# Neighbourhood attention on one Trainium2 core: a head's bias joins its mask by an accumulating transfer instead of an addition on GpSimd

## The chip, the core and the metric

The kernel runs on one core of one Trainium2 chip. The metric is the device time of one execution in microseconds (us); less is better. The core has TensorE (PE in the profile; PEld is its weight load), VectorE (DVE), ScalarE (ACT), GpSimd (POOL) and SyncE (SP). SP, ACT and POOL can issue transfers (DMAs), which 16 DMA engines carry out.

## What is computed

One pre-norm encoder block in float32 on 512 tokens of width 2048: a combined input projection, two attention mixers side by side (eight heads of latent attention, MLA, and eight heads of neighbourhood attention on an 8 by 64 grid), an output projection, a squared-ReLU MLP of width 8192 and a last norm. The change is in the neighbourhood attention, whose reference is, cut to what matters:

```
def na_mixer(q, k, v, rpb):
    ...
    dr = rs + jnp.arange(kr) - r + (NA_ROWS_MAX - 1)
    bias = rpb[:, dr[:, None, None], dc[None, :, :]]
    ...
    s = jnp.einsum('bchd,bicjhd->bhcij', qr, kw, ...) * scale
    s = (s + bias[None]).reshape(B, H, W, kr * kc)
    p = jax.nn.softmax(s, axis=-1)...
    return jnp.einsum('bhcij,bicjhd->bchd', p, vw)
```

A query sees 16 columns of all 8 grid rows, with a learned bias for each relative position and head.

## The kernel before, in words

The tokens are laid out column by column, so that a block of 128 queries covers 16 grid columns and needs at most 256 keys. The window is a mask of zeros and -1e30 with three variants (left edge, middle, right edge): a constant array `mask` of 128 x 3 x 256 numbers. The bias of a head is one 128 x 256 array; all eight lie in a DRAM tensor `b_d`, which 8 + 16 transfers on POOL's queue put together from the weights at the start (lines 277 and 279).

For each head `na_load` (from line 440) fetches the head's q, k and v blocks, its bias into `bt` (line 451) and the mask into `bm` (line 453), all from SP's queue, and GpSimd then adds the bias to each of the three mask variants, in place in `bm` (line 454). `bt` and `bm` have one buffer each. `na_steps` then works on four query blocks. Step `s1`: the score matmul (line 470), then VectorE scales the scores and adds `bm` (line 472), takes the row maximum (475), ScalarE exponentiates (476), VectorE takes the reciprocal and normalises (477, 478). Step `s2` transposes the probabilities on TensorE (483) and ScalarE copies them out (485). Step `s3` multiplies them with v (492); after the fourth block `finish_head` scales the head's output, and GpSimd adds its squares to a running sum (509).

The order is made by hand and then by the framework. By hand: the heads' steps are tasks, and `hook()` runs those that are due after each product of a Strassen-like projection (`strassen_t`, lines 305 to 307, seven products for each of twelve weight blocks, 24 matmuls of 256 columns each). A head's load is due three hooks ahead of its first `s1`, its blocks follow every second hook, and `s2` comes two or three hooks after `s1`. So the attention runs in the gaps of the projection, from about 107 to 404 us; the last two heads lie beside the MLA set-up (lines 549 to 594: transposes of the latents, rope, and the projections `mq`, `mk`, `mvp` of lines 102 to 104). Then, when the kernel is built, the framework fixes one order for each engine and each queue: it takes what it estimates to be ready first, earlier statements before later ones, and puts in the waits. Each engine works through its own list in order, so one that waits holds up all that stands behind it.

Helpers have one line for all callers: `split` writes each float32 operand as a high and a low part (ACT line 92, DVE line 93), `TT` is a VectorE operation on two tensors (line 204), and `raw_unit` is a weight load (line 77).

Of the kernel before, what the change touches and what calls it, by code (L numbers as in the profile page):

```python
# [10 lines left out]
F32 = mybir.dt.float32  # L11
F32R = mybir.dt.float32r
AF = mybir.ActivationFunctionType
ALU = mybir.AluOpType
# [3 lines left out]
P = 128  # L18
# [18 lines left out]
def block_kernel(ctx, tc, x, xT, w_c, w_ckv, w_qkv, w_uqn, w_uqr, w_ukv, rpb, gcols, w_out, w_ff1, w_ff2, g_fin,  # L37
                 cs, mask, out):
    nc = tc.nc
# [4 lines left out]
    def open_pool(name, bufs=1, **kw):  # L44
        e = ExitStack()
        p = e.enter_context(tc.tile_pool(name=name, bufs=bufs, **kw))
        stacks[name] = e
        return p
# [166 lines left out]
    for k in range(KH):  # L215
        xt = load_xT(k) if k else xt0
        for j in range(2):
            sc = nc.vector.scalar_tensor_tensor(out=xt[:, 2 * j:2 * j + 2], in0=xt[:, 2 * j:2 * j + 2],
                                                scalar=gc[:, G_IN + k + KH * j:G_IN + k + KH * j + 1],
                                                in1=rB3 if k else rt_.rearrange("p (b n) -> p b n", b=2), op0=ALU.mult, op1=ALU.mult)  # L220
# [50 lines left out]
    b_d = tc.dram_tile([P, H, 256], F32, name="b_d")  # L271
# [6 lines left out]
    for ql in range(16):  # L278
        nc.gpsimd.dma_start(out=b_d[ql * 8:(ql + 1) * 8],
                            in_=g_d[:, :, 15 - ql:47 - ql, :].rearrange("q h c r -> q h (c r)"))  # L280
# [148 lines left out]
    na = open_pool("na", side="left")  # L429
# [10 lines left out]
    def na_load(h):  # L440
        p, h2 = h // 2, h % 2
        if p == 3:
            qT, kT = (last[w][:, h2 * S:(h2 + 1) * S] for w in range(2))
        else:
            qT, kT = (na.tile([P, S], F32, name=f"n{t}{h}", tag=f"n{t}", bufs=1) for t in "qk")
            nc.sync.dma_start(out=qT, in_=q_d[p][:, h2 * S:(h2 + 1) * S])
            nc.sync.dma_start(out=kT, in_=k_d[p][:, h2 * S:(h2 + 1) * S])
        vn = na.tile([P, NM, P], F32, name=f"nvn{h}", tag="nv", bufs=2)
        nc.sync.dma_start(out=vn, in_=v_d[p].rearrange("p (m d) -> p m d", m=NM)[:, :, h2 * P:(h2 + 1) * P])
        bt = na.tile([P, 256], F32, name=f"bt{h}", tag="bt", bufs=1)  # L450
        nc.sync.dma_start(out=bt, in_=b_d[:, h, :])
        bm = na.tile([P, 3, 256], F32, name=f"bm{h}", tag="bm", bufs=1)
        nc.sync.dma_start(out=bm, in_=mask)
        nc.gpsimd.tensor_tensor(out=bm, in0=bm, in1=bt.unsqueeze(1).broadcast_to([P, 3, 256]), op=ALU.add)
        return h, qT, kT, vn, bm

    def na_steps(h, t0, gap):
        d = {}

        def start():  # L460
            d["in"] = na_load(h)
# [723 lines left out]
```

## Time and profile before

| what | us |
|---|---|
| median of 3 runs | 1959.23 (1957.66 to 1959.66) |
| the profiled execution | 1961.26 |
| its span, first to last instruction | 1959.50 |
| what lies around the span | 1.76 |
| TensorE busy | 1941.2 (99%) |
| VectorE busy | 1567.3 (80%) |
| ScalarE busy | 1004.3 (51%) |
| GpSimd busy | 63.2 (3%) |
| DMA queue of SP, share of 16 engines | 41.4% |

The profile records one execution. Busy shares are means over the whole span; waits and the timeline tell what a stretch is limited by. In the timeline a row has the start, the duration, the engine, the line, the operation, and output <- inputs; the bracket at its end is the idle time of the engine ahead of it and what ended that. Matmuls overlap, so their durations are longer than their spacing.

### The profile page before, as it was taken

What the parts mean: (1) busy time and instruction counts of PE and PEld (TensorE: products, weight loads), DVE (VectorE), ACT (ScalarE), POOL (GpSimd) and SP (SyncE); (2) the same over time, 40 slices, a digit from 0 to 9 for tenths busy, and PEclk for the clock granted to TensorE, in tenths of its full rate; (3) what the DMA queues carried; (4) which work ended last, traced back from release to release, by engine and by line L of the source; (5) the groups of instructions that cost most, each with busy time, mean ns of one, the idle gap of its engine ahead of it and who ended that gap; (6) DMA issues with size and microseconds to landing.
All of it is one profiled execution on the core that took longest, in us unless ns stands there. A gap on an engine that the chain in (4) does not pass through costs nothing.

```text
span 1959.5 us, 31084 instructions
## 1 busy us (share of the span) xinstructions
PE 1941.2 (99%) x12510; PEld 1765.3 (90%) x12510; DVE 1567.3 (80%) x1894; ACT 1004.3 (51%) x1436; POOL 63.2 (3%) x69
## 2 busy tenths in 40 slices
PE   9999999999999999999999999999999999999998
PEld 8999999888887899999999999998888888888886
DVE  8677777787535687787878787875899999999996
ACT  5654555575314555555555555555454454454443
POOL 2100010100000000000000000000000000000000
PEclk9999999999999999999999999999999999999999
DMA  8354554431334344545454545357355345444433
GB/s 285 131 195 142 174 165 149 138 113 49 101 120 164 127 151 140 173 145 179 142 182 140 183 135 189 130 168 251 129 189 174 132 161 165 168 161 132 159 134 135
DMA packets 121936, 303.75 MB, mean 155 GB/s; under 512 B 10816, under 2 KB 49728, under 8 KB 121536
## 3 DMA queue, kind: packets, MB, share of 16 engines
q1 hardware_dynamic: 98416, 271.09, 41.4%
q10 hardware_dynamic: 22608, 29.52, 4.2%
q8 instruction: 98, 1.61, 0.3%
q0 software_dynamic: 768, 1.15, 0.2%
q14 instruction: 46, 0.38, 0.1%
HBM read 250.60 MB, written 52.26 MB: 155 GB/s over the span
## 4 chain that ended last, share of the span: by engine, by line
PE 94%; DVE 2%; ACT 1%; DMA 1%; issue 1%; POOL 0%; POOLq 0%; DVEq 0%; ACTq 0%; SPq 0%
PE px L307 8%; PE px L306 8%; PE px L305 8%; PE sx L1000 5%; PE sx L1002 5%; PE sx L1001 5%; PE pz L307 4%; PE pz L306 4%; PE pz L305 4%; PE wo L104 3%; PE wo L102 3%; PE wo L103 3%; PE sz L1000 3%; PE sz L1002 3%; PE sz L1001 3%; PE py L307 2%
## 5 line engine op out<-in xcount | busy, mean ns | idle before, releaser
L92 ACT CAST op_a<-sb 128x1024 fp32r<-128x1024 f32 x58 | 61.1, 1053 | 61.7 <-PE sx L1002 23.8
L93 DVE TENSOR_TENSOR op_a<-sb,op_a 128x1024 fp32r<-128x1024 f32 x58 | 70.3, 1217 | 6.6 <-ACT op_a L92 6.6
L204 DVE TENSOR_TENSOR SF<-SF,sx 128x1024 f32<-128x1024 f32 x56 | 67.9, 1212 | 0.6 <-PE sx L1002 0.6
L204 DVE TENSOR_TENSOR sb<-sb,sb 128x1024 f32<-128x1024 f32 x56 | 67.1, 1218 | 0.5
L92 ACT CAST s_0hi<-sb 128x1024 fp32r<-128x1024 f32 x28 | 29.5, 1055 | 42.6 <-PE sx L1002 16.8
L127 POOL TENSOR_TENSOR stat<-stat,nhalf 128x1 f32<-128x1 f32 (+1 forms) x6 | 7.3, 1217 | 1355.7 <-DVE stat L126 1355.7
L92 ACT CAST a_0hi<-sb 128x1024 fp32r<-128x1024 f32 x27 | 28.5, 1055 | 35.1 <-PE sz L1002 16.6
L886 ACT ACTIVATE v<-v 128x512 f32<-128x512 f32 x64 | 40.4, 631 | 3.1 <-DVE v L204 2.2
L887 ACT ACTIVATE v<-v 128x512 f32<-128x512 f32 x64 | 40.6, 634 | 1.9
L92 ACT CAST a_1hi<-sb 128x1024 fp32r<-128x1024 f32 x27 | 28.4, 1051 | 23.3 <-PE sz L1002 10.0
L93 DVE TENSOR_TENSOR a_0lo<-sb,a_0hi 128x1024 fp32r<-128x1024 f32 x27 | 32.9, 1219 | 8.8 <-ACT a_0hi L92 8.8
L92 ACT CAST s_1hi<-sb 128x1024 fp32r<-128x1024 f32 x28 | 29.4, 1050 | 17.0 <-PE sx L1002 16.7
L204 DVE TENSOR_TENSOR b<-b,b 128x1024 f32<-128x1024 f32 x31 | 37.6, 1214 | 0.0
L93 DVE TENSOR_TENSOR s_0lo<-sb,s_0hi 128x1024 fp32r<-128x1024 f32 x28 | 34.1, 1218 | 1.5 <-ACT s_0hi L92 1.4
L204 DVE TENSOR_TENSOR SF<-SF,sz 128x1024 f32<-128x1024 f32 x28 | 34.0, 1214 | 0.4 <-PE sz L1002 0.4
L204 DVE TENSOR_TENSOR sb<-st,sb 128x1024 f32<-128x1024 f32 x28 | 34.1, 1217 | 0.0
L204 DVE TENSOR_TENSOR st<-sb,sb 128x1024 f32<-128x1024 f32 x28 | 34.1, 1217 | 0.0
L93 DVE TENSOR_TENSOR s_1lo<-sb,s_1hi 128x1024 fp32r<-128x1024 f32 x28 | 34.1, 1216 | 0.0
L93 DVE TENSOR_TENSOR wo_2lo<-wo_2r,wo_2hi 128x1024 fp32r<-128x1024 f32 x8 | 9.8, 1224 | 28.9 <-ACT wo_2hi L92 27.2
L93 DVE TENSOR_TENSOR a_1lo<-sb,a_1hi 128x1024 fp32r<-128x1024 f32 x27 | 32.9, 1217 | 0.0
L476 ACT ACTIVATE pb<-pb,nst 128x192 f32<-128x192 f32 (+1 forms) x32 | 15.5, 484 | 33.7 <-DVE nst L475 33.7
L93 DVE TENSOR_TENSOR mpt<-mt,mpt 128x512 fp32r<-128x512 f32 x32 | 22.0, 687 | 12.2 <-ACT mpt L92 12.1
(3929 smaller groups left out, 8229.2 us busy)
## 6 DMA issues: line engine op xcount, KB each, us to landing
sb<-in_w_ff_dram SPq DMA_DIRECT2D x112, 512.0 KB, 5.0
b<-in_w_ff_dram SPq DMA_DIRECT2D x64, 512.0 KB, 6.0
f_d<-v ACTq DMA_DIRECT2D x32, 512.0 KB, 6.9
s_d<-sv SPq DMA_DIRECT2D x28, 512.0 KB, 6.6
nb<-in_w_qkv_dram SPq DMA_DIRECT2D x24, 512.0 KB, 4.8
xn<-in_x_dram SPq DMA_DIRECT2D x8, 512.0 KB, 5.6
X<-in_x_dram SPq DMA_DIRECT2D x16, 256.0 KB, 5.6
wo_0r<-in_w_out_dram SPq DMA_DIRECT2D x8, 512.0 KB, 4.2
```

The source lines that it names most:

```text
L92: i = nc.scalar.copy(hi, src)
L93: nc.vector.tensor_tensor(out=lo, in0=src, in1=hi.bitcast(F32), op=ALU.subtract)
L102: nc.tensor.matmul(ps, ah, bh, start=first, stop=False)
L103: nc.tensor.matmul(ps, ah, bl, start=False, stop=False)
L104: nc.tensor.matmul(ps, al, bh, start=False, stop=last)
L204: nc.vector.tensor_tensor(out=out, in0=a, in1=b, op=op)
L305: nc.tensor.matmul(ps, bh, ah, start=first and kk == 0, stop=False, **kw)
L306: nc.tensor.matmul(ps, bh, al, start=False, stop=False, **kw)
L307: nc.tensor.matmul(ps, bl, ah, start=False, stop=kk == 7, **kw)
L1000: nc.tensor.matmul(ps[:, mm], ah, bh, start=first and kk == 0, stop=False, **kw)
L1001: nc.tensor.matmul(ps[:, mm], ah, bl, start=False, stop=False, **kw)
L1002: nc.tensor.matmul(ps[:, mm], al, bh, start=False, stop=kk == 2 * nu - 1, **kw)
```

## The change

`bt`, its load from SP and the addition on GpSimd go. In their place GpSimd issues one transfer for each head that reads the head's bias from DRAM three times over (a broadcast of the source) and adds it to `bm` as it arrives. The mask's load stays as it is, and the transfer has to wait for it.

```diff
         vn = na.tile([P, NM, P], F32, name=f"nvn{h}", tag="nv", bufs=2)
         nc.sync.dma_start(out=vn, in_=v_d[p].rearrange("p (m d) -> p m d", m=NM)[:, :, h2 * P:(h2 + 1) * P])
-        bt = na.tile([P, 256], F32, name=f"bt{h}", tag="bt", bufs=1)
-        nc.sync.dma_start(out=bt, in_=b_d[:, h, :])
         bm = na.tile([P, 3, 256], F32, name=f"bm{h}", tag="bm", bufs=1)
         nc.sync.dma_start(out=bm, in_=mask)
-        nc.gpsimd.tensor_tensor(out=bm, in0=bm, in1=bt.unsqueeze(1).broadcast_to([P, 3, 256]), op=ALU.add)
+        nc.gpsimd.dma_start(out=bm, in_=b_d[:, h, :].unsqueeze(1).broadcast_to([P, 3, 256]), accum_op=ALU.add)
         return h, qT, kT, vn, bm
```

## Rows read from the trace of the kernel before

**Rows 1.** The page's first part: busy time and share of each engine.
```profile
PE 1941.2 (99%) x12510; PEld 1765.3 (90%) x12510; DVE 1567.3 (80%) x1894; ACT 1004.3 (51%) x1436; POOL 63.2 (3%) x69
```

**Rows 2.** Busy time by stretch: length, PE, PEld, DVE, ACT, POOL, PEclk, DMA share, GB/s.
```profile
100.00:410.00 310.00, 306.93 (x2427) 296.46 (x2426) 240.10 (x362) 161.46 (x301) 28.57 (x18) 1.00 0.47 154
```

**Rows 3.** Waits of PE from 100 to 410 us: total, times, longest.
```profile
PE mvp L102 <- DVE mks L93: 1.7, 1, 1.7
...
PE nt L483 <- DVE pb L478: 0.4, 1, 0.4
```

**Rows 4.** Groups of POOL by line: count, busy, mean ns, idle time before.
```profile
L454 POOL TENSOR_TENSOR bm<-bm,bt 128x768 f32<-128x768 f32 x8 | 18.0, 2256 | 216.3 <-DMA bm<-in_mask_dram 184.4 <-DVE ob_12lo L93 31.9
L277 POOL DMA_DIRECT2D g_d<-in_rpb_dram x8 | 5.0, 627 | 0.0
```

**Rows 5.** Waits of DVE (from 100 to 410 us) and of SP's queue (all).
```profile
DVE pb L472 <- POOL bm L454: 4.2, 3, 1.4
...
SPq L451 <- POOL bm L454: 32.9, 7, 6.5
```

**Rows 6.** Timeline around the second head's first block: SP, POOL, DVE, PE.
```profile
189.62 0.32 SPq L451 DMA_DIRECT2D bt<-b_d  x1
193.83 0.33 SPq L77 DMA_DIRECT2D nb_22r<-in_w_qkv_dram  x1
...
187.22 2.37 POOL L454 TENSOR_TENSOR bm<-bm,bt 128x768 f32<-128x768 f32 x1 [74.33 <-DMA bm<-in_mask_dram]
...
189.63 0.36 DVE L472 SCALAR_TENSOR_TENSOR pb<-ns,bm 128x192 f32<-128x192 f32 x1 [1.39 <-POOL bm L454]
192.55 1.22 DVE L204 TENSOR_TENSOR nt<-nb_11r,nt 128x1024 f32<-128x1024 f32 x1
193.69 0.31 DVE L478 TENSOR_SCALAR pb<-pb,nst 128x192 f32<-128x192 f32 x1
...
197.85 0.38 PE L483 MATMUL nt<-ident,pb 128*128 128x128 f32 x2
```

**Rows 7.** Timeline of POOL and DVE at the fifth head.
```profile
283.15 2.45 POOL L454 TENSOR_TENSOR bm<-bm,bt 128x768 f32<-128x768 f32 x1 [15.63 <-DMA bm<-in_mask_dram]
...
283.93 2.75 DVE L204 TENSOR_TENSOR nt<-nb_23r,nt 128x1024 f32<-128x1024 f32 x1
...
299.90 0.36 DVE L472 SCALAR_TENSOR_TENSOR pb<-ns,bm 128x192 f32<-128x192 f32 x1
```

**Rows 8.** Timeline at the seventh head: POOL, DVE, PE.
```profile
351.68 1.84 POOL L454 TENSOR_TENSOR bm<-bm,bt 128x768 f32<-128x768 f32 x1 [15.13 <-DMA bm<-in_mask_dram]
...
356.08 0.35 DVE L472 SCALAR_TENSOR_TENSOR pb<-ns,bm 128x192 f32<-128x192 f32 x1
357.62 0.50 DVE L478 TENSOR_SCALAR pb<-pb,nst 128x192 f32<-128x192 f32 x1
...
358.23 0.39 PE L483 MATMUL nt<-ident,pb 128*128 128x128 f32 x2
```

**Rows 9.** Timeline at the eighth head: POOL, DVE, PE; and all of L585.
```profile
377.25 1.85 POOL L454 TENSOR_TENSOR bm<-bm,bt 128x768 f32<-128x768 f32 x1 [19.25 <-DMA bm<-in_mask_dram]
...
380.44 0.68 DVE L93 TENSOR_TENSOR mks<-mk,mks 128x512 fp32r<-128x512 f32 x1
387.58 0.35 DVE L472 SCALAR_TENSOR_TENSOR pb<-ns,bm 128x192 f32<-128x192 f32 x1
...
381.18 0.38 PE L102 MATMUL mvp<-wk0hi,ckv 128*128 128x256 f32 x1 [1.66 <-DVE mks L93]
...
L585 DVE TENSOR_TENSOR qrn<-qrn,rt x8: 404/416/1877, 364.4 to 377.5; 128x256 f32<-128x256 f32 x8
```

**Rows 10.** DMA issues: engine, operation, count, KB each, median us from issue to landing.
```profile
bm<-in_mask_dram SPq DMA_DIRECT2D x8, 384.0 KB, 3.6
...
b_d<-g_d POOLq DMA_DIRECT2D x16, 64.0 KB, 4.6
...
bt<-b_d SPq DMA_DIRECT2D x8, 128.0 KB, 2.4
```

## The prediction

> **What bounds the kernel now.** I read the page's busy shares first: TensorE is busy 99% of the span, GpSimd 3% [rows 1]. So the addition on GpSimd isn't scarce work in itself; it can matter only where TensorE waits for something behind it. Next, the table by stretch: all eight additions lie between 100 and 410 us, where TensorE is busy for 306.93 of 310 us [rows 2]. The 3.07 us left are the most that a smoother attention could give back, 0.16% of the time, if a busy TensorE has nothing else to give. Then the waits of TensorE in that stretch: one of 1.7 us for VectorE (the low part `mks` of an MLA key), and one of 0.4 us for a normalised probability block, are what touches this change [rows 3]. The groups of GpSimd give eight additions of 2256 ns on average, each after the mask's load [rows 4]. Last, the waits of VectorE and of SP's queue [rows 5], and the timeline head by head [rows 6 to 9], which shows who stands behind each addition.
>
> The times are summed against the profiled execution (1961.26 us, span 1959.50); the median of the runs shown is 1959.23, so 2.03 is taken off at the end.
>
> **What is removed.** Eight loads of `bt`, 0.32 us each on SP's queue [rows 6]. At seven of them the queue had also waited for the previous addition, 32.9 us in all [rows 5]: `bt` has one buffer, so the next head's load stands in SP's list just behind the mask's and waits until the addition has read the last one. That looks like a prize, but what stands behind it is late for another reason: after the `bt` load at 189.62 the next transfer starts only at 193.83, just after VectorE has finished with the weight buffer that it refills (192.55 plus 1.22 is 193.77) [rows 6]. Gain on TensorE's path: nothing; the cover is that weight buffer, and SP's wait is next put down to it.
>
> The eight additions go too. For heads 1, 3 and 5 the addition is ready long ahead of its reader: at head 5 it starts at 283.15 and the first block reads `bm` at 299.90 [rows 7]. But it slows VectorE. A two-tensor operation that takes 1.22 us elsewhere [rows 6] took 2.75 us beside it [rows 7], 1.53 more. TensorE doesn't wait there, so that is worth nothing on the path; VectorE has 69.90 us free in the stretch (310 less 240.10) [rows 2]. At head 8 it does count: line 585 took 1.877 us beside the addition, where its median is 0.416 [rows 9]. That is 1.46 us, and the `mks` part behind it on VectorE came at 380.44 and held TensorE for 1.66 us until 381.18 [rows 9]. Without the addition, 1.46 of this 1.66 goes: **-1.5**. Next late is then the same `mks` part, 0.2 us behind.
>
> **What is added.** Eight transfers on GpSimd's queue, behind the same wait for the mask. To write them, GpSimd is occupied for about 0.63 us each, if a transfer of many short pieces on that queue is the measure (627 ns) [rows 4]. That is less than 2256, and the other work in its list, the sums of line 509, comes no later. The bias is read three times, 384 KB a head in place of 128 [rows 10], and the destination as well; eight heads of this at a DMA share of 0.47 [rows 2] cost nothing, since nothing on the path waits for bandwidth.
>
> What counts is the delay from the point where the addition starts now to the point where `bm` is complete; call it X. Now X is 2.41 us at head 2 (187.22 to 189.63) [rows 6]. No row shows an accumulating transfer. The least is 2.4, the `bt` load itself, from the same source by SP's queue; the most that I take is 7.8, the mask's load of the same tile and bytes twice over, since every byte is read on both sides (2 x 3.6), and 0.63 for GpSimd [rows 4, 10]. The nearest row is the one queue that shares the way of issuing: 64 KB transfers of POOL's queue land 4.6 us after issue [rows 10]. They carry a sixth of the bytes but write to DRAM. I take a little more, **X = 5.0**. The Trainium skill, "DMA: Bandwidth & Descriptors", section "Anatomy of one DMA — SWDGE (gpsimd) path", gives a fixed 2.0 us and the bytes at 436 GB/s; for 393 KB that is an estimate of 2.9 us, and the sum would then be -1.5 alone. The row of 4.6 us for a sixth of the bytes speaks against it.
>
> The room for X, head by head:
> - Heads 2, 4 and 6 (the three waits of 1.4 us in [rows 5]; head 2 stands for all): VectorE already waits for `bm` at 189.63, and all of X beyond 2.41 delays it and its list. TensorE needs the block first at 197.85, for the transposes, and it is normalised at 193.69 plus 0.31, at 194.00 [rows 6]. So 3.85 us of room; X may reach 6.3. At 5.0: 0 each, hidden by that lead; without it, each would cost 2.6.
> - Head 7: the addition starts at 351.68, VectorE reads at 356.08, so X may be 4.40. From there nothing is spare: the block is normalised at 357.62 plus 0.50, and the transposes follow at 358.23, after the 0.4 us of waiting in [rows 3, 8]. At 5.0: **+0.6**, in full, since the MLA operands stand behind it on VectorE.
> - Head 8: 377.25 to 387.58, 10.3 us of room [rows 9]: 0. Heads 1, 3 and 5: more [rows 7]: 0.
>
> Sum: -1.5 + 0.6 = -0.9; 1961.26 becomes 1960.4, and the median 1959.23 becomes **1958.3**. A measurement of this kernel can tell about 0.2%, or 3.9 us, from no change, so this is "no change".
>
> **The rivals.**
> *A slow transfer (slower).* X is 7.8, as bounded above. Heads 2, 4 and 6 then lack 7.8 - 6.26 = 1.5 us each, 4.6 together; head 7 lacks 3.4; head 8 still gives 1.5: +6.5, so 1965.7. In general the sum is 4X - 24.6 from X = 6.3 up; it passes +3.9 at X = 7.2. For it: 384 KB are added onto 384 KB, and a plain load takes 3.6 us [rows 10]. Against it: the landing of a plain load is largely a fixed cost, as `bt` takes 2.4 us for a third of the bytes [rows 10]; doubling only the part that grows with the bytes (3.6 - 2.4, over 256 KB, is 1.8 for 384 KB) gives 3.6 + 1.8 + 0.63 = 6.0, still below. The Trainium skill has the rule in "Collectives: The Full Stack", section "The bandwidth ceiling: the fold count and why AG ≠ RS ≠ AR": an addition in the transfer reads two sources and runs at half the rate of a copy. No run here shows it yet. Chance 0.18.
>
> *GpSimd gets in VectorE's way all the same (no change).* Writing the transfer's list may hold VectorE as the addition does. With the 1.5 us at head 8 gone and X = 5.0, the sum is +0.6, 1959.8. For it: the cause of the 2.75 us in [rows 7] is only known to be the addition beside it. Against: 0.63 us instead of 1.84. Chance 0.16.
>
> *The order is laid out anew (faster).* The framework sorts each engine's list by its own estimates, and the attention operations move to other places. If that cleared every wait of the stretch, it would give 3.07 us [rows 2], 1956.2, still within 0.2%; more would need shorter gaps between matmuls that are counted as busy. A bad order has no such limit, but each misplaced operation costs about what head 7 or 8 shows, 0.4 to 1.7 us [rows 3]. Chance of a gain of over 0.2%: 0.05.
>
> **The numbers.** The forecast has 0.61, the slow transfer 0.18, GpSimd in the way 0.16, the new order 0.05. Slower by over 0.2% is the slow transfer alone, 0.18; faster by that much 0.05; within it 0.61 + 0.16 = 0.77. The lower end is 1956.0, all of TensorE's waits gone; the upper is 1965.0, X at 7.6, which leaves out the tail of the slow transfer.
>
> **What would show it.** Right: VectorE still waits for `bm` at heads 2, 4 and 6, now for a transfer and some 2.6 us longer each, with TensorE's waits unchanged there; the `mks` wait of 1.7 us shrinks to some 0.2; a wait of TensorE for line 478 at head 7 grows from 0.4 to about 1; SP no longer waits at line 451; no VectorE operation of 2.75 us beside GpSimd's issue. It is wrong if the transfer takes over 6.3 us, when waits of TensorE for line 478 appear at three more heads; if the long VectorE operations stay; or if the lists are sorted so differently that heads 7 and 8 aren't the tight ones any more.

## The result, and the profile after

The changed kernel takes 1968.69 us (median of 6 runs, 1965.12 to 1970.71), the kernel before 1958.83 in 6 runs on the same chip: a ratio of 1.0052, 95% interval 1.0041 to 1.0063. It is slower by 9.9 us; forecast was 1958.3, with a range up to 1965.0. Behind the edit all line numbers of the kernel after are two lower: the accumulating transfer is line 452, the read of `bm` on VectorE 470, the exponential 474, the transposes 481, the copy `npt` 483, its use on TensorE 490.

The profiled executions differ by less, 1968.15 against 1961.26. The one of before lost some 1.6 us at 714 to 718 us to a granted clock of 0.50 and 0.72, which the one of after didn't (both in the last part of this section). Without that they are 8.5 us apart.

Nearly all that differs lies in the attention's stretch. First the busy shares of the kernel after, then the stretch of [rows 2] (length, PE, PEld, DVE, ACT, POOL, PEclk, DMA share, GB/s), and TensorE's waits there (total, times, longest):

```profile
PE 1942.2 (99%) x12510; PEld 1764.8 (90%) x12510; DVE 1561.9 (79%) x1894; ACT 1004.1 (51%) x1436; POOL 55.7 (3%) x69
```
```profile
100.00:410.00 310.00, 301.59 (x2377) 291.16 (x2376) 228.78 (x347) 155.65 (x288) 18.52 (x16) 0.99 0.52 158
```
```profile
PE no L490 <- ACT npt L483: 5.0, 4, 2.0
PE ns L468 <- DMA nk<-k_d: 1.4, 1, 1.4
PE nt L481 <- DVE pb L476: 1.3, 2, 0.9
```

GpSimd and VectorE have less to do (63.2 to 55.7, 1567.3 to 1561.9 us), and TensorE is idle for longer: 8.41 us of the stretch where it was 3.07. The `mks` wait of 1.7 us of [rows 3] is gone. In its place stands a wait that no row of before has: TensorE waits four times, 5.0 us in all, for ScalarE's copy `npt` of transposed probabilities. Next, what answers to [rows 5]: VectorE's waits, and those of SP's queue.

```profile
DVE pb L470 <- DMA bm<-b_d: 11.6, 3, 4.3
...
SPq L77 <- DVE nt L204: 69.8, 9, 13.0
```

VectorE's three waits for `bm` have grown from 4.2 to 11.6 us. SP no longer waits for the addition; the 32.9 us have gone to the weight loads behind, waiting for VectorE to free a buffer (34.4 us in the profile of before, now 69.8). Now the timeline of the second head's first block (start, duration, engine, line, operation, and in brackets the idle time ahead):

```profile
186.94 0.61 PE L490 MATMUL no<-npt,nvn 128*128 128x128 f32 x4
...
187.51 1.28 POOL L452 DMA_DIRECT2D bm<-b_d  x1 [76.14 <-DVE nt L204]
...
190.70 1.05 ACT L92 CAST ot_11hi<-nb_11r 128x1024 fp32r<-128x1024 f32 x1 [2.15 <-PE px L306]
193.17 0.36 DVE L470 SCALAR_TENSOR_TENSOR pb<-ns,bm 128x192 f32<-128x192 f32 x1 [4.30 <-DMA bm<-b_d]
...
194.95 0.45 ACT L474 ACTIVATE pb<-pb,nst 128x192 f32<-128x192 f32 x1 [3.21 <-DVE nst L473]
195.41 0.35 ACT L483 COPY npt<-nt 128x256 f32<-128x256 f32 x1
195.81 0.71 PE L490 MATMUL no<-npt,nvn 128*128 128x128 f32 x4 [2.01 <-ACT npt L483]
```

And the same place in the kernel before:

```profile
187.44 0.61 PE L492 MATMUL no<-npt,nvn 128*128 128x128 f32 x4
...
191.41 0.46 ACT L476 ACTIVATE pb<-pb,nst 128x192 f32<-128x192 f32 x1 [2.37 <-DVE nst L475]
...
191.87 1.03 ACT L92 CAST ot_11hi<-nb_11r 128x1024 fp32r<-128x1024 f32 x1
...
192.81 0.36 ACT L485 COPY npt<-nt 128x256 f32<-128x256 f32 x1
...
194.14 0.61 PE L492 MATMUL no<-npt,nvn 128*128 128x128 f32 x4
```

X, from the transfer's start on GpSimd to the read of `bm`, is 193.17 - 187.51 = 5.66 us (5.59 at head 4, 5.66 at head 6), where the addition took 2.41. In ScalarE's list the second head's exponential stands ahead of the copy `npt`, and that copy isn't the second head's: it holds the transposed probabilities of the *first* head's last block, which TensorE needs for that head's product with v. Before, the copy ended at 193.17 and TensorE used it at 194.14: 0.97 us of room. After, it ends at 195.76, and TensorE has stood still for 2.01 us.

Both kernels have the product of the block before as a mark on TensorE (186.94 after, 187.44 before). Counted from it, `bm` is read 6.23 us on, where it was 2.19; call this D. It is 4.04 more: 3.25 of it is X, and the rest stands ahead of X (against the mark the mask landed 0.45 us later, and the transfer starts 0.56 us behind that landing where the addition started 0.22 behind it). TensorE waits for 2.01 of the 4.04. The room of 0.97 accounts for a half of the difference. The other is in the list: before, a cast of the projection (`ot_11hi`, 1.03 us) stood between exponential and copy; now the framework has put it ahead of the exponential, where it runs while ScalarE waits anyway.

Then the seventh and the eighth head, as in [rows 8, 9]:

```profile
360.67 1.30 POOL L452 DMA_DIRECT2D bm<-b_d  x1 [15.95 <-DVE wr1lo L93]
...
366.65 0.36 DVE L470 SCALAR_TENSOR_TENSOR pb<-ns,bm 128x192 f32<-128x192 f32 x1 [1.80 <-PE ns L468]
367.07 0.66 PE L559 MATMUL krt<-ident,krsr 128*128 128x128 f32 x4 [0.42 <-DVE pb L470]
368.59 0.44 PE L481 MATMUL nt<-ident,pb 128*128 128x128 f32 x2 [0.86 <-DVE pb L476]
...
388.72 0.68 DVE L93 TENSOR_TENSOR mks<-mk,mks 128x512 fp32r<-128x512 f32 x1
```

At head 7, X is 5.98. The bracket at 366.65 names a score matmul; it is the second block's, the first block's having been through at 364.57, so the transfer is what is left: it landed 5.9 us after its start, just ahead of the read. The transposes come at 368.59, 10.36 later than at 358.23 [rows 8]. The `mks` part comes 8.28 later than at 380.44 [rows 9]: about 2 us have been won back in between.

Last, the clock after such a stop. Stretches of 2 us of the kernel after, at the second head, and a later stop and the stretch behind it:

```profile
194.00:196.00 2.00, 0.19 (x1) 0.19 (x2) 2.00 (x4) 1.05 (x5) 0.00 (x0) 1.00 0.00 0
197.00:199.00 2.00, 2.00 (x12) 2.00 (x11) 2.00 (x6) 0.22 (x1) 0.00 (x0) 0.54 0.90 279
199.00:201.00 2.00, 2.00 (x13) 2.00 (x12) 1.41 (x2) 1.52 (x5) 0.00 (x0) 0.60 0.86 179
...
722.00:724.00 2.00, 2.00 (x19) 2.00 (x19) 1.97 (x3) 1.11 (x2) 0.00 (x0) 1.00 0.83 256
```
```profile
720.11 0.39 PE L305 MATMUL px<-op_b,ot_0hi 128*128 128x256 f32 x1 [1.16 <-ACT ot_0hi L92]
721.37 0.39 PE L307 MATMUL px<-op_b,ot_0lo 128*128 128x256 f32 x1 [0.76 <-DVE ot_0lo L93]
```

The same later stop in the kernel before, and the stretches behind it:

```profile
711.81 0.39 PE L305 MATMUL px<-op_b,ot_0hi 128*128 128x256 f32 x1 [1.16 <-ACT ot_0hi L92]
713.07 0.39 PE L307 MATMUL px<-op_b,ot_0lo 128*128 128x256 f32 x1 [0.76 <-DVE ot_0lo L93]
```
```profile
714.00:716.00 2.00, 2.00 (x11) 2.00 (x11) 1.97 (x3) 1.02 (x1) 0.00 (x0) 0.50 0.81 262
716.00:718.00 2.00, 2.00 (x14) 2.00 (x14) 2.00 (x3) 0.47 (x2) 0.00 (x0) 0.72 0.00 0
```

After TensorE's stop at 194 to 196 us the granted clock falls to 0.54 and 0.60 (the lower level, 1.2 GHz of 2.4, for most of 4 us). By these shares up to 2 x 0.46 + 2 x 0.40 = 1.7 us more are lost; the matmuls show 1.5, as 16 of them follow at 0.21 us instead of 0.12 (from 197.15 to 200.52 us). The later stop, 1.16 and 0.76 us, is the same in both kernels, and it has such a fall behind it only in the profile of before.

**Where the 9.9 us come from.** Both kernels run the same projection products in the same order, so the start of the n-th on TensorE can be compared. The kernel after is 0.5 us ahead up to the second head; then it loses 3.8 there (the stop and the clock), 1.3 at the third head (the late `nk`), 2.0 at the fourth, 2.1 at the sixth, 1.7 at the seventh, and wins 1.9 back at the eighth: 9.0 in all, and 8.5 behind by 410 us. That is all of what the profiled executions differ by when the fall at 714 us is left out; the other 1.4 us of the medians lie within the spread of the runs.

### The profile page after: what moved, and what is told of

Its sections match the earlier page's. It is cut to its first block, busy times and chain, and to the rows that moved or that the text cites. A ratio compares the mean times of both kernels' runs of the same rounds, so it can differ in the third digit from the quotient of the medians.

```text
span 1966.3 us, 31079 instructions
## 1 busy us (share of the span) xinstructions
PE 1942.2 (99%) x12510; PEld 1764.8 (90%) x12510; DVE 1561.9 (79%) x1894; ACT 1004.1 (51%) x1436; POOL 55.7 (3%) x69
## 4 chain that ended last, share of the span: by engine, by line
PE 93%; DMA 2%; DVE 2%; issue 1%; ACT 1%; POOL 0%; SPq 0%; POOLq 0%; ACTq 0%; DVEq 0%
PE px L307 8%; PE px L306 8%; PE px L305 8%; PE sx L999 5%; PE sx L998 5%; PE sx L1000 5%; PE pz L307 4%; PE pz L306 4%; PE pz L305 4%; PE wo L102 3%; PE wo L104 3%; PE wo L103 3%; PE sz L999 3%; PE sz L998 3%; PE sz L1000 3%; PE py L307 2%
## 5 line engine op out<-in xcount | busy, mean ns | idle before, releaser
L93 DVE TENSOR_TENSOR a_0lo<-sb,a_0hi 128x1024 fp32r<-128x1024 f32 x27 | 32.9, 1219 | 8.8 <-ACT a_0hi L92 8.8
L470 DVE SCALAR_TENSOR_TENSOR pb<-ns,bm 128x192 f32<-128x192 f32 (+1 forms) x32 | 12.4, 388 | 24.5 <-PE ns L468 12.7
```

What stands on the lines that cost most here:

```text
L93: nc.vector.tensor_tensor(out=lo, in0=src, in1=hi.bitcast(F32), op=ALU.subtract)
```

## The experiments

**The theory:** the transfer completes `bm` later than the addition did, and at heads 2, 4 and 6 the delay passes through VectorE and ScalarE's ordered list to the copy that TensorE needs for the head before. **The rivals:** the transfer costs by its traffic (three reads of the bias, both sides of the addition); or the time goes to a list sorted differently. Each run is compared with the kernel before on its own chip, which took 1958.98 us there; beside the first run below, the three tiles and the sum in DRAM it took 1959.35. Each profile is one execution.

### The copy ahead of the exponential

```diff
-            late = 1 if h < 6 else 0
+            late = 1 if h < 6 and i < 3 else 0
```

> The changed kernel, with the fourth block's step s2 two hooks after s1 instead of three, so that ScalarE's copy (line 483) of a head's fourth block stands in its list ahead of the next head's exponential (line 474). Delay theory (the transfer is about 5.6 us behind the mask, the next head's first block waits for it on VectorE, its exponential waits for VectorE, and the copy behind that exponential keeps TensorE waiting): TensorE's waits of 5.0 us for the copy of line 483 go, and with them most of 6 us (2.3 + 1.5 + 1.7 + 2.1 by the timeline, less what then shows up elsewhere): 1961 to 1964. VectorE still waits some 3.6 to 4.3 us at heads 2, 4 and 6. Rival, the transfers' traffic slows everything: no change, 1967 to 1970. Rival, VectorE's own delay starves TensorE of low parts: waits for line 93 take the place of those for line 483, 1967 to 1970.

1964.1 us; ratio 1.0028, 1.0019 to 1.0038. The last block's transposes and copy come one hook earlier, ahead of the next head's exponential. TensorE's waits:

```profile
PE nt L481 <- DVE pb L476: 2.3, 5, 0.9
PE no L490 <- ACT npt L483: 2.3, 4, 0.8
PE krt L559 <- DVE pb L470: 1.7, 1, 1.7
```

VectorE still waits for `bm` as long as in the kernel after (4.3 us at the longest), but `no` waits 2.3 instead of 5.0 us, none over 0.8, and half of the loss is back. The gain is a little below what was expected (1961 to 1964, with no wait for the copy). So the copy's place in the list is a part of the price. The other half appears elsewhere: the transposes wait for `pb` five times, and head 7 (whose `krt` stands behind the same late block) more than in the kernel after. Making room in one list moved the tight place to the next. The profiled execution is the slowest of the ten (1967.09 us): at 365 to 369 us it also has a fall of the clock like the one above.

### The addition kept at four heads

```diff
-        nc.gpsimd.dma_start(out=bm, ..., accum_op=ALU.add)
+        if h in (1, 3, 5, 6):
+            bt = na.tile([P, 256], F32, name=f"bt{h}", tag="bt", bufs=1)
+            nc.sync.dma_start(out=bt, in_=b_d[:, h, :])
+            nc.gpsimd.tensor_tensor(out=bm, in0=bm, in1=bt..., op=ALU.add)
+        else:
+            nc.gpsimd.dma_start(out=bm, ..., accum_op=ALU.add)
```

> Heads 1, 3, 5 and 8 with the accumulating transfer as in the changed kernel, heads 2, 4, 6 and 7 with bt and GpSimd's addition as before. Delay theory: the loss sits at heads 2, 4, 6 and 7, where the next reader stands close behind, so it is gone; the wait of 1.4 us for nk at head 3 shows whether the transfer's traffic has a price of its own there: 1957 to 1961, as before. Traffic theory: half of the transfers remain and so does half of the loss: 1963 to 1965.

1958.58 us; ratio 0.9992, 0.9983 to 1.0001. All the loss is gone with four transfers (heads 1, 3, 5 and 8) still in place. VectorE's waits for `bm`:

```profile
DVE pb L475 <- POOL bm L455: 4.2, 3, 1.4
```

These are the 4.2 us of [rows 5] again. TensorE has the 0.4 us of [rows 3] for the transposes left, no wait for `npt` or `nk`, and none at `mvp` (head 8 has the transfer, and with it the gain). The loss sits at heads 2, 4, 6 and 7.

### The same transfer without the addition

```diff
-        nc.gpsimd.dma_start(out=bm, ..., accum_op=ALU.add)
+        nc.gpsimd.dma_start(out=bm, ...)
```

> The changed kernel with the same transfer, behind the same wait, but overwriting bm in place of adding to it: the mask is left out of the sum. It measures what adding costs over copying. If adding halves the rate, bm is there 1.5 to 2 us earlier (3.6 to 4 us behind the mask), the waits of VectorE fall to some 2 us each and the time to 1959 to 1963. If the way of issuing is what takes the time, the landing stays near 5.6 us and the time at 1966 to 1970.

1962.6 us; ratio 1.0020, 1.0011 to 1.0029. The mask is left out of the sum here. The second head:

```profile
187.67 0.61 PE L490 MATMUL no<-npt,nvn 128*128 128x128 f32 x4
...
187.84 0.77 POOL L452 DMA_DIRECT2D bm<-b_d  x1 [76.49 <-DMA bm<-in_mask_dram]
...
192.63 0.36 DVE L470 SCALAR_TENSOR_TENSOR pb<-ns,bm 128x192 f32<-128x192 f32 x1 [3.00 <-DMA bm<-b_d]
...
195.28 0.71 PE L490 MATMUL no<-npt,nvn 128*128 128x128 f32 x4 [0.75 <-ACT npt L483]
```

X is 4.79 (4.62 and 4.84 at heads 4 and 6). So at these heads the addition itself costs 0.8 to 1.0 us of X, half a microsecond of it in GpSimd's issuing (0.77 against 1.28). Adding doesn't double the time of a copy: that would have been 1.5 to 2 us, with the plain transfer there after 3.6 to 4. The time lies in the range expected for doubling, but because the price isn't proportional to X. Over all eight heads, most of them with other transfers in flight, the landing takes 4.5 to 7.7 us (median 5.1) without the addition and 5.5 to 9.5 (median 6.5) with it. `bm` that comes 0.8 to 1.0 us sooner at three heads gives 6 of the 9.9 us back: TensorE waits 0.75, 0.25 and 0.30 us for the copy, the clock doesn't fall there, and `nk` isn't waited for. From the first score matmul to the 24th matmul of `mvp` this execution is 2.1 us longer than before's (223.5 for 221.4); the rest of the 3.6 wasn't traced.

### The delay without a transfer

```diff
         nc.gpsimd.tensor_tensor(out=bm, in0=bm, in1=bt.unsqueeze(1).broadcast_to([P, 3, 256]), op=ALU.add)
+        nc.gpsimd.tensor_scalar(out=bm, in0=bm, scalar1=1.0, scalar2=None, op0=ALU.mult)
+        nc.gpsimd.tensor_scalar(out=bm, in0=bm, scalar1=1.0, scalar2=None, op0=ALU.mult)
```

> The kernel before with GpSimd's addition followed by two passes over bm that multiply it by 1.0 (some 1 us each), so that bm comes later without any transfer. Delay theory: VectorE's three waits for bm at heads 2, 4 and 6 grow from 1.4 us by the passes' time, TensorE's wait for line 485 (the copy behind the exponential) appears as soon as the delay passes about 1 us there, and the time rises by 2 to 7 us. Traffic theory: no transfer was added, so no change beyond what GpSimd takes from VectorE: 1957 to 1960.

1977.94 us; ratio 1.0094, 1.0080 to 1.0107: slower by 19 us, where 2 to 7 were expected. The passes took 2.1 to 3.0 us each, longer than assumed, so X became 6.31, 7.09 and 7.10. GpSimd and VectorE, and then TensorE, at the second head:

```profile
187.40 0.61 PE L494 MATMUL no<-npt,nvn 128*128 128x128 f32 x4
187.78 1.84 POOL L454 TENSOR_TENSOR bm<-bm,bt 128x768 f32<-128x768 f32 x1 [69.58 <-DMA bm<-in_mask_dram]
...
194.09 0.36 DVE L474 SCALAR_TENSOR_TENSOR pb<-ns,bm 128x192 f32<-128x192 f32 x1 [5.87 <-POOL bm L456]
...
196.33 1.03 ACT L92 CAST ot_11hi<-nb_11r 128x1024 fp32r<-128x1024 f32 x1
197.26 0.36 ACT L487 COPY npt<-nt 128x256 f32<-128x256 f32 x1
197.68 0.71 PE L494 MATMUL no<-npt,nvn 128*128 128x128 f32 x4 [3.43 <-ACT npt L487]
```

With no transfer of the change in it, the kernel shows the same wait at the same place, and a longer one. D is 6.69, 0.46 more than in the kernel after; the wait is 1.42 longer, because here the cast stands behind the exponential again, as in the kernel before. The profiled execution is the fastest of four (1975.21 us), so its rows don't account for all of the 19 us. Since X overshot, half of the delay was tried:

### Half of that delay

The same, with one pass.

> The kernel before with one GpSimd pass that multiplies bm by 1.0 behind the addition, where the run with two passes had X of 6.3 to 7.1 us at heads 2, 4 and 6 and lost 19 us. A pass took 2.1 to 3.0 us there, so X should be 4.4 to 5.0 at these heads, as it was (4.6 to 4.8) with the transfer that doesn't add, which lost 3.6 us. Theory (what counts is when bm is complete; nothing of the transfer itself costs time): slower by 2 to 6 us, 1961 to 1965, with waits of TensorE for the copy npt at line 486 or near it of 0.5 to 1 us at heads 2, 4 and 6. Rival (the loss of 3.6 us with the plain transfer was in part its traffic): within 1.5 us of the kernel before, although VectorE waits for bm by some 3 us three times.

1966.07 us; ratio 1.0036, 1.0021 to 1.0050. The second head, and the eighth:

```profile
186.25 0.61 PE L493 MATMUL no<-npt,nvn 128*128 128x128 f32 x4
186.38 2.02 POOL L454 TENSOR_TENSOR bm<-bm,bt 128x768 f32<-128x768 f32 x1 [71.35 <-DMA bm<-in_mask_dram]
...
190.65 0.36 DVE L473 SCALAR_TENSOR_TENSOR pb<-ns,bm 128x192 f32<-128x192 f32 x1 [3.62 <-POOL bm L455]
...
194.24 0.71 PE L493 MATMUL no<-npt,nvn 128*128 128x128 f32 x4 [1.14 <-ACT npt L486]
...
386.37 0.58 PE L102 MATMUL mvp<-wk0hi,ckv 128*128 128x256 f32 x1 [2.25 <-DVE mks L93]
```

X is 4.27, 4.63 and 4.52, and `no` waits 1.14 us at each of heads 2, 4 and 6. The wait follows D as it does with the transfers (the table in the next section), so no traffic is needed to explain it; the rival's "within 1.5 us" is out. The time is slower by 7.1 us, more than the 2 to 6 expected: at head 8 the `mks` wait of [rows 3] grew by 0.6, from 1.66 to 2.25 us, and here the granted clock fell behind it (0.84, 0.50 and 0.80 in three stretches of 2 us from 385 on, at most 1.7 us): together about a third of the 7.1.

### A transfer for each variant

```diff
-        nc.gpsimd.dma_start(out=bm, in_=b_d[:, h, :].unsqueeze(1).broadcast_to([P, 3, 256]), accum_op=ALU.add)
+        for v in range(3):
+            nc.gpsimd.dma_start(out=bm[:, v], in_=b_d[:, h, :], accum_op=ALU.add)
```

> The changed kernel with three accumulating transfers for a head, one for each mask variant (128 KB each), the first block's variant first; the mask's load is still one. If the landing grows with the bytes, the first variant is there clearly earlier than 5.6 us (4 us, say), the waits of VectorE at heads 2, 4 and 6 shrink by as much (from 3.6 to 4.3 to some 2.2) and the time falls to 1961 to 1965. If the landing is a fixed cost (nearly all of 5.6 us), the time stays at 1967 to 1970. Traffic theory: slower than the changed kernel, as GpSimd issues three times as often.

1958.53 us; ratio 0.9995, 0.9987 to 1.0004: better than the 1961 to 1965 expected, and no slower than the kernel before. A head's first block needs the first variant alone, and it is there sooner:

```profile
187.19 0.61 PE L491 MATMUL no<-npt,nvn 128*128 128x128 f32 x4
...
187.40 2.65 POOL L453 DMA_DIRECT2D bm<-b_d  x3 [73.90 <-DMA bm<-in_mask_dram]
...
190.64 0.36 DVE L471 SCALAR_TENSOR_TENSOR pb<-ns,bm 128x192 f32<-128x192 f32 x1 [1.53 <-issue]
```

D is 3.45 (3.99 at head 4, 3.18 at head 6). TensorE's waits for `no` and `mvp` are both gone; the same bytes move as in the kernel after, by the same queue, in three times as many transfers. So the loss hangs on when the first variant is ready, not on how much is moved.

### Three tiles, with the transfer and with the addition

```diff
-        bm = na.tile([P, 3, 256], F32, name=f"bm{h}", tag="bm", bufs=1)
...
+        bm = []
+        for v, (o, n) in enumerate(((64, 192), (0, 256), (0, 192))):
+            m = na.tile([P, n], F32, name=f"bm{v}_{h}", tag=f"bm{v}", bufs=1)
+            nc.sync.dma_start(out=m, in_=mask[:, v, o:o + n])
+            nc.gpsimd.dma_start(out=m, in_=b_d[:, h, o:o + n], accum_op=ALU.add)
+            bm.append(m)
```

The second kernel has `bt` and GpSimd's addition in the same loop. A variant's tile is free once the blocks that read it are through, so the next head's first variant loads while the head before still works.

> The changed kernel with the mask in three tiles (192, 256 and 192 columns, only those that are read), each loaded and added to by a transfer of its own; a tile comes free as soon as its last block has been read, so that the next head's loads can go out early. Delay theory: no wait of VectorE for bm is left, the loss at heads 2, 4, 6 and 7 goes and the gain at head 8 (the low part of mks no longer held up beside GpSimd's addition, 1.9 us) stays: 1956 to 1959, as the kernel before or 1 to 2 us less. Traffic theory (contention on the DMA engines or with GpSimd's issuing): still 1964 or more, since more transfers are issued.

> The kernel before with the same three tiles, and the addition on GpSimd. Delay theory: the three waits of 1.4 us go, but TensorE did not pay for them; 1957 to 1960, as before, the addition still slows VectorE beside it. If the three tiles gain by themselves (by the order that they bring) it shows here, and then the gain of the three tiles with transfers is not the transfers'.

With the transfer 1957.76 us, ratio 0.9998 (0.9989 to 1.0007); with the addition 1957.77, ratio 0.9991 (0.9982 to 1.0000). The stretch of [rows 2] in the first:

```profile
100.00:410.00 310.00, 308.43 (x2433) 297.82 (x2432) 236.65 (x370) 162.99 (x303) 31.77 (x34) 1.00 0.53 157
```

Where `bm` is early in either way, VectorE doesn't wait for it, and transfer and addition are the same within the measurement. Neither is told apart from the kernel before: of the 3.07 us that TensorE was idle in this stretch, 1.57 are left (1.31 in the second), and a gain of 1.5 to 1.8 us is below what the measurement can tell.

### The sum made once, in DRAM

```diff
+    m_d = tc.dram_tile([P, H, 3, 256], F32, name="m_d")
+    for h in range(H):
+        nc.gpsimd.dma_start(out=m_d[:, h], in_=mask)
+    for h in range(H):
+        nc.gpsimd.dma_start(out=m_d[:, h], in_=b_d[:, h, :]..., accum_op=ALU.add)
...
-        nc.sync.dma_start(out=bm, in_=mask)
-        nc.gpsimd.dma_start(out=bm, ..., accum_op=ALU.add)
+        nc.sync.dma_start(out=bm, in_=m_d[:, h])
```

> The sums of mask and bias of all heads are made once in DRAM at the start, by 8 plain and 8 accumulating transfers on GpSimd's queue, and each head loads its sum by one transfer on SP's queue; no addition and no second wait is left for a head. Delay theory: 1956 to 1959, unless the 6 MB more at the start delay the first loads (up to 100 us the DMA share is 0.62, so some us may be lost there). Traffic theory: slower than the changed kernel, as more bytes are moved.

1963.26 us; ratio 1.0028, 1.0017 to 1.0039. The attention's stretch has no wait for `bm`, but the first 100 us pay for it. Here, and in the kernel before:

```profile
0.00:100.00 100.00, 93.55 (x504) 82.97 (x505) 73.99 (x118) 54.41 (x86) 32.82 (x50) 0.97 0.81 247
```
```profile
0.00:100.00 100.00, 97.32 (x539) 87.38 (x540) 77.49 (x124) 59.62 (x95) 19.63 (x35) 1.00 0.61 210
```

TensorE is busy for 3.77 us less there, at a DMA share of 0.81 for 0.61 and a lower granted clock. From 55 to 90 us no weight load of line 77 took over 3.8 us to land before; here two took 8.5 and 10.3, and ScalarE waited 6.3 us for the first of them. So in a stretch that already loads the first weights, traffic does cost; how much of the loss is the clock's wasn't separated. At heads 2, 4 and 6, where the transfer runs almost alone (70 to 74 GB/s, about its own bytes), no such price showed.

## Why the prediction was wrong

**The cause in one table.** D is the time from the mark on TensorE (the product with v of the block before) to the read of `bm`, and the wait is TensorE's for the copy, both at heads 2, 4 and 6. The last column is the difference of medians on the same chip. The upper four have the cast of the projection behind the exponential in ScalarE's list, the lower three ahead of it.

| kernel | D, us | wait, us | us over before |
|---|---|---|---|
| before | 2.19, 2.19, 2.21 | 0 | 0 |
| addition at four heads | 2.19, 2.20, 2.21 | 0 | -0.4 |
| addition and one pass | 4.40, 4.41, 4.41 | 1.14, 1.14, 1.14 | +7.1 |
| addition and two passes | 6.69, 6.62, 6.65 | 3.43, 3.35, 3.39 | +19.0 |
| transfer for each variant | 3.45, 3.99, 3.18 | 0 | -0.5 |
| plain transfer | 4.96, 4.47, 4.49 | 0.75, 0.25, 0.30 | +3.6 |
| after | 6.23, 5.64, 5.54 | 2.01, 1.42, 1.33 | +9.9 |

Wherever TensorE waits, D less the wait is 3.26 or 3.27 in the upper part and 4.19 to 4.22 in the lower: the wait is what D has over a fixed room, whether a transfer or GpSimd brings the delay, and the two rooms differ by the cast (1.03 us, less a little overlap). That settles the mechanism at these heads. The whole time isn't given by the waits alone: the falls of the clock, the third head and the eighth come on top (with one pass, the eighth head and the clock behind it are about a third of the 7.1).

Point by point, by the prediction's steps:

- *What bounds the kernel.* As read: TensorE, and its waits in the stretch. The most to be won, 3.07 us, stood; the best runs won about half of it in TensorE's idle time, and that is below what the measurement tells.
- *The loads of `bt` and SP's wait.* As forecast, nothing; the 32.9 us moved to the weight loads behind.
- *Head 8, -1.5.* As forecast: the `mks` wait is gone (0.2 us of it was to stay), and TensorE gains 1.9 us there.
- *X = 5.0.* It measured 5.6 at heads 2, 4 and 6 and 6.0 at head 7, within the bounds of 2.4 and 7.8. GpSimd's part was 1.30 us, not 0.63. The estimate of 2.9 us by the Trainium skill, "DMA: Bandwidth & Descriptors", section "Anatomy of one DMA — SWDGE (gpsimd) path", was low even for the transfer without an addition (4.6 to 4.8).
- *Heads 2, 4 and 6, "3.85 us of room; X may reach 6.3".* **This is the step that failed.** The room was read along the new head's own chain: its block is normalised at 194.00 and transposed at 197.85. But the exponential that `bm` holds up stands in ScalarE's list ahead of another head's copy, and that had 0.97 us. With it X could reach 2.41 + 0.97 = 3.4, not 6.3. The sign that was named for this step, a transfer of over 6.3 us with waits for line 478, didn't show: the transfer stayed below it there, and the new waits were for the copy. The three heads lost 3.8 + 2.0 + 2.1 = 7.9 us where 0 was forecast, 1.5 of it by the clock; without the cast's new place it would have been about 0.95 more at each.
- *Head 7, +0.6.* The mechanism was right, the term too small: X of 5.98 over 4.40 is 1.6, and the head lost 1.7.
- *Not in the sum at all:* the clock's fall behind the stop at head 2 (1.5), and the wait for `nk` at head 3 (1.4). The second is explained in part. The load of `nk` waits until `k_d`, the write of the keys to DRAM, has landed; that took 7.8 us, and 6.9 to 7.5 in the three other profiles with an accumulating transfer in flight beside it at head 3, against 4.7 to 6.0 in those without one. So the transfer's traffic seems to have a part in it. But where head 3 keeps the transfer and heads 2, 4 and 6 don't, the load itself landed in 3.3 us instead of 5.3, and TensorE didn't wait. The wait was seen in one execution; its cause stays open.

The rivals: *a slow transfer* gave 1965.7 and the right sign, but by an X of 7.8 and a wait of the transposes, and both were otherwise (its 4X - 24.6 passes +3.9 at 7.1, not at 7.2). The rule weighed there, that an addition in the transfer reads two sources and runs at half the rate of a copy, is what the Trainium skill, "Collectives: The Full Stack", section "The bandwidth ceiling: the fold count and why AG ≠ RS ≠ AR", states of the reduce step of a ring collective at large sizes. It isn't borne out for this transfer: 0.8 to 1.0 us on 4.75. *GpSimd in VectorE's way* is refuted: at head 5 GpSimd issues from 290.04 to 291.34 us, and the operation beside it that took 2.75 us before [rows 7] takes its usual time:

```profile
290.50 1.22 DVE L204 TENSOR_TENSOR nt<-nb_23r,nt 128x1024 f32<-128x1024 f32 x1
```

*A new order* was real, but small and on the good side: the cast's new place spared 0.95 us at three heads.

Had the room been read as 0.97 us, the forecast with its own X of 5.0 would have been -1.5 + 0.6 + 3 x 1.6 = +3.9, 1963.1. That is still short of the 1968.7; the rest is the larger X at four heads, the clock and head 3, with the cast's new place against it.

## What to carry to other kernels

Taking work off an engine that is idle 97% of the time gains little by itself (here 1.9 us at one head, where that work had slowed VectorE); what counts is when its result is there, and a transfer that replaces a short operation may be later although no engine works for it. The room for such a delay must be read on every engine's ordered list that the late value passes through: not only "when is this block needed next" but "what stands behind the instruction that it holds up, and who needs that", even if it belongs to other work. Here the loss went without a faster transfer: by asking for less first (one variant of three) or by freeing the buffer sooner.

## What was not expected of the hardware

- An accumulating transfer of 384 KB onto on-chip memory occupied GpSimd for 1.30 us, the plain one 0.78, and at heads 2, 4 and 6, where they ran almost alone, they were ready in 5.6 and 4.75 us from the start of issuing. A third of the bytes was ready there in 3.2 to 4.1 us, so more than half of the time doesn't go by the byte. With other transfers in flight the landing took up to 9.5 us (plain: 7.7).
- The same stop of TensorE (1.16 and 0.76 us, some 1.3 us apart) was followed by a fall of the granted clock in one profiled execution and not in another. At the second head 2.01 us of waiting brought 1.5 more by the clock, so there the late value cost three quarters more than its wait. With two passes such a fall followed the stops at heads 2 and 4 (3.43 and 3.35 us) and not the one at head 6 (3.39).
- A GpSimd pass with one input over 128 x 768 numbers took 2.1 to 3.0 us, no less than the addition with two inputs, 2.3.
